# Norm steps only beside attention slots, a ring of five value quarters, six bias-table buffers, and bulk transfers on the Pool queue, in an eight-core transformer layer

## The chip, the cores and the metric

The kernel runs on all 8 cores of one Trainium2 chip; each core computes two of the sixteen sequences. The metric is the device time, in microseconds, of the slowest core. Cores 0 to 3 form die 0, cores 4 to 7 die 1. Some executions are slow on one die or on both, at a lower granted clock: in the profiled run of the kernel before, die 0 took 4469.6 us at a clock of 0.892, die 1 4179.2 us at 0.982.

## The reference, cut to what matters

One encoder layer: a gated feed-forward half step, two attention mixers side by side on one normalised input, a gated merge, a second feed-forward half step and a final norm.

```python
BATCH, SEQ, D_MODEL, D_FF = 16, 2048, 1024, 2816

def reference(x, ...):
    x = x + 0.5 * swiglu(rmsnorm(x, norm_ffn1[l]), ffn1_gate[l], ffn1_up[l], ffn1_down[l])
    h = rmsnorm(x, norm_mix[l])
    proj = h @ w_in[l]
    da_q, da_k, da_v, sw_q, sw_k, sw_v, gate = jnp.split(proj, splits, axis=-1)
    # ... lam from da_lambda ...
    o_da = diff_attention(...)      # dense, 8 heads of 2x64, ALiBi bias, values 128 wide
    o_sw = window_attention(...)    # band of +-128 tokens, 16 query heads, sink
    g = jax.nn.sigmoid(gate.reshape(B, S, 2, D_MODEL) + b_gate[l])
    merged = g[:, :, 0] * (o_da @ w_proj_da[l]) + g[:, :, 1] * (o_sw @ w_proj_swa[l])
    x = x + merged @ w_out[l]
    x = x + 0.5 * swiglu(rmsnorm(x, norm_ffn2[l]), ffn2_gate[l], ffn2_up[l], ffn2_down[l])
    return rmsnorm(x, norm_final)
```

## The kernel before

Activations lie as 8 blocks of 512 tokens (blocks 0 to 3 are the first sequence of the core, 4 to 7 the second). The program is a fixed list of stages. In the first half: GU (gate and up matmuls), D (down) and W (the projection), for pairs of blocks at first, then for single blocks. In the second half, per block: P (attention projections and gates), O (output projection), GU and D. I write O3 for block 3 in stage O. Blocks 4 to 7 pass through GU and D in both halves: below, GU4 to GU7 and D4 to D7 are those of the first half, and GU0 to GU3, D2 and D3 those of the second. The function `build` walks through *boundaries* between groups of matmuls. At each boundary it can put in three other kinds of work: an **attention slot**, a **norm step**, and the issue of **queued transfers** ("doling"). Attention runs in two spans, from the middle of W(2,3) to W7, and from W7 to P4.

```python
    def build(self):                        # cut
        span = [(at("W", (2, 3), 1) + 32, w7 + 12), (w7 + 18, at("P", (4,), 2) - 6)]
        for si, (k, bl, ph) in enumerate(st):
            inside = any(a <= n < b for a, b in span)
            self.gset = [6, 7] if inside else [6, 7, 0, 1, 2, 3, 4, 5]   # PSUM banks for the matmul groups
            self.rate = 2 if k == "D" and len(bl) == 1 else 1
            for _ in self.begin(k, bl, ph):
                n += 1
                # ...
                self.pre()                  # a norm step that needs the PE, if one is due
                for q, (a, b) in enumerate(span):
                    if n == a - (10, 6)[q]:
                        # ...
                        self.first_loads(q) # queues the first q, k, v, bias-table ... loads of a span
                    if a < n <= b:
                        want = int(total * (q + (n - a) / (b - a)) + 1e-6)
                        if done < want:
                            self.hint_group(k)          # the early wait, see below
                        while done < want:              # the attention slot
                            next(steps)
                            done += 1
                # ...
                self.post()                 # up to `rate` norm steps that need no PE
                self.dole()                 # issues queued transfers
            self.end(k, bl, ph)

    def hint_group(self, k):                # PE waits here for what the NEXT matmul group needs
        r, w = [], []
        t = "d" if k == "D" else "a"
        if self.taken[t] < self.issued[t]:
            r.append(("r" + t, self.taken[t] % self.nslot[t]))           # its weights
        if self.open is None:
            w.append(("bk", self.gset[self.gi % len(self.gset)]))        # its PSUM bank
        self.S.hint("pe", r, w)

    def dole(self):                         # dq[0]: attention's loads, dq[1]: everything else
        for _ in range(2 if len(self.dq[0]) > 2 else 1):
            q = self.dq[0] or self.dq[1]
            if q:
                q.pop(0)[1]()
```

A norm is a generator. Each `yield` is a step; `yield "pe"` announces a step that puts matmuls on the PE. If a stage needs the norm before its steps are used up, it is *drained*: all that is left runs at once and the PE waits for it.

```python
    def norm(self, ri, gi, hi=None, store=None, need=None):
        for c in range(8):                  # ACT squares, DVE sums: nacc
            # ...
            yield
        self.copy("dve", self.nh, self.nacc, ["nacc"], ["nh"])           # high and low bf16 parts
        self.tt(self.nl, self.nacc, self.nh, ALU.subtract, ["nacc", "nh"], ["nl"])
        yield
        yield "pe"
        b, bk = self.bank()
        # ... 8 matmuls of nh, nl with ones: sums over 128 partitions -> bank
        self.ts(self.ms, b[:, 0:4], 1.0 / 1024.0, 1e-6, ALU.mult, ALU.add, [bk], ["ms"])
        self.tt(self.r4, self.ms, self.mhalf, ALU.pow, ["ms", "mhalf"], ["r4"], eng="pool")
        # ... rh, rl = high and low parts of r4
        yield
        yield "pe"
        b, bk = self.bank()
        # ... 8 matmuls that broadcast rh, rl -> bank
        self.copy("act", self.nrb, b, [bk], ["nrb"])
        yield
        for c in range(8):                  # DVE: R * gain * nrb
            # ...
            yield

    def end(self, k, bl, ph):               # cut
        if k == "O" and b not in (3, 7):
            self.bg.append(self.norm(b % 2, 2, 0))
            if self.late:                   # final norms wait here for the next O
                self.bg += self.late
                self.late = []
        if k == "D":
            if b in (0, 1):
                self.late.append(self.normf(b))
```

Values and bias tables:

```python
    self.vD = sb("vD", [128, 16, 129], ...)               # one head's values, four quarters of 2x2 tiles
    def b_av(...):                                        # after the last use of a quarter by a head:
            if qb == 3 and c == 1 and u < 7:
                self.load_vD(sq, u + 1, bt)               # the next head's quarter goes to the same place

    self.tst = [sb("tst%d" % i, [128, 496], BF16, ...) for i in range(2)]
    for j in range(8):                                    # start of the program: 64 table pieces
        for h in range(8):
            self.act(self.tst[n % 2], self.dd, AF.Exp, ["dd"], [("tst", n % 2)], scale=-sl)
            self.dma(self.td_d[h][:, 496 * j:496 * (j + 1)], self.tst[n % 2], ...)
```

The softmax here doesn't subtract the row's maximum and nothing guards it: scores larger than these inputs give would overflow.

## Time and profile before

| quantity | before |
|---|---|
| time, median of 6 runs | 4199.47 us (4191.19 to 4222.8) |
| core 5: span, PE busy | 4183.4 us, 3932.1 us (94%) |
| core 5: PE idle before matmuls, all gaps summed | 242.4 us |
| core 5: time lost at half clock | 27 episodes, 81 us |

A half-clock episode is a stretch in which the clock record of the core stands at 0.5; half of its length is counted as lost. The views of waits below leave out gaps under 0.15 us.

The first view gives each core's span and mean granted PE clock. The profiled run was slow on die 0, so that die is not read.

```profile
core 5: 4183.4 us, clock 0.981
...
die 0 (median of its cores): 4469.6 us, clock 0.892
die 1 (median of its cores): 4179.2 us, clock 0.982
```

I read core 5: its trace holds all 27236 matmuls. From here on every profile line is of core 5 unless another is named. Its busy times (with share and instruction count), from the page:

```profile
PE 3932.1 (94%) x27236; PEld 2014.3 (48%) x27236; DVE 2374.2 (57%) x4565; ACT 1864.9 (45%) x2572; POOL 180.1 (4%) x247
```

PE bounds the kernel (it is busy for 94% of core 5's span and takes 76% of the chain that ended last), so I count a wait of PE's own as time on the critical path. The view of waits lists what ended them: total us, times, longest us.

```profile
PE bank L373 <- DVE nh L394: 32.3, 7, 10.4
...
PE bank L373 <- DVE of L382: 14.5, 3, 13.9
PE bank L373 <- DVE ms L388: 12.9, 13, 1.9
...
PE bank L373 <- DMA vD<-vd_d: 9.9, 5, 2.5
PE bank L373 <- ACT nrb L376: 9.2, 10, 1.0
...
PE bank L373 <- DMA H_64<-h_d: 8.5, 2, 7.8
...
PE bank L373 <- DMA qS<-qs_d: 2.2, 1, 2.2
```

The names: `nh` is the high part of a norm's sum of squares, `ms` its mean square, `nrb` the factor that the norm broadcasts, `of` a final norm's output, `vD` attention's values, `H` the normalised input, `qS` queries of the window mixer. The waits for `ms` and `nrb` come after norm steps. This is one of them in the timeline (start, us busy, engine, line, output and inputs; in brackets the idle time and what ended it):

```profile
2587.32 0.16 PE L373 MATMUL bank<-onesb,nh 128*128 128x1 bf16 x1 [1.02 <-DVE fr_79 L382]
...
2589.13 1.02 PE L373 MATMUL bank<-vD,et_104 128*128 128x129 bf16 x8 [1.46 <-DVE ms L388]
```

The sum matmuls start at 2587.32. The next thing that PE does is attention (`vD`, `et`), which has no use for `ms`. It waits all the same, since the early bank wait of `hint_group` stands ahead of the slot, and the bank is in use by the norm until `ms` has been read from it.

The 13.9 us wait for `of` is a drain. On DVE, at the head of stage O3:

```profile
2989.65 4.72 DVE L382 SCALAR_TENSOR_TENSOR R_62<-R_62,gains,nrb 128x512 f32<-128x512 f32 x7
3005.56 0.69 DVE L382 SCALAR_TENSOR_TENSOR R_62<-bank,R_62 128x512 f32<-128x512 f32 x1 [11.19 <-DMA R_62<-x_d]
```

Seven of the eight final multiplications of block 1's final norm run at once; only then can that buffer be stored and block 3's data be loaded into it, and DVE waits 11.19 us for the load.

For stages, the table of windows: window, its length, busy time of each engine (with counts), mean granted clock, DMA share, GB/s. A stage begins at the first matmul that uses a weight tile of that stage. DMA share is the mean busy share of the core's 16 DMA engines. The rows are the stages GU(0,1), W(2,3), P1, O1 and O3.

```profile
27.66:221.50 193.84, 165.16 (x721) 70.09 (x721) 78.06 (x128) 70.51 (x132) 12.98 (x23) 0.95 0.68 159
672.81:855.57 182.76, 175.34 (x1347) 102.64 (x1345) 90.44 (x174) 86.89 (x119) 11.09 (x18) 0.97 0.83 181
2228.95:2337.42 108.47, 95.41 (x767) 49.73 (x765) 70.47 (x140) 65.22 (x88) 3.37 (x3) 0.97 0.39 119
2530.55:2554.47 23.92, 22.75 (x187) 11.91 (x185) 17.95 (x40) 10.95 (x12) 1.01 (x1) 1.00 0.63 175
2987.23:3029.14 41.91, 26.62 (x206) 13.35 (x204) 24.32 (x49) 13.06 (x18) 1.01 (x1) 0.84 0.61 205
```

PE is busy only 165 of 194 us in GU(0,1), and 27 of 42 in O3. Finally, the sync engine's queue in W(2,3), where the first attention span begins (`kD` is attention's first load, `qS` the first load of queries for the window mixer):

```profile
717.15 1.39 SPq L401 DMA_DIRECT2D kD<-kd_d  x2
...
736.60 2.75 SPq L401 DMA_DIRECT2D vD<-vd_d  x2
...
747.32 0.46 SPq L401 DMA_DIRECT2D qS<-qs_d  x1
```

From the first load to `qS` it takes 747.32 − 717.15 = 30.2 us.

### The profile page before, as it was taken

To read this page: it belongs to the slowest core of one execution; us is meant where nothing else is said; L and a number is where in the kernel's file an instruction comes from. 1 tells how busy PE (TensorE), PEld (TensorE's weight loads), DVE (VectorE), ACT (ScalarE), POOL (GpSimd) and SP (SyncE) were. 2 spreads that over 40 slices of the span, in tenths; PEclk is the share of its full clock that TensorE was granted. 3 is DMA by queue.
4 is the path that set the end of the run, shared out by engine and by line. 5 is a ranking of instruction groups with operands and counts; after the bars stand their busy time and mean duration, and the time that the engine had idled before them with its cause. 6 is when DMAs were issued, how large, how long until landed. Compare 5 with 4: busy or idle time off the path is not lost.

```text
span 4509.8 us, 76897 instructions; the slowest of 8 cores (4170.2 to 4509.8 us)
## 1 busy us (share of the span) xinstructions
PE 4277.1 (95%) x27236; PEld 2123.1 (47%) x27236; DVE 2379.9 (53%) x4565; ACT 1867.9 (41%) x2572; POOL 180.2 (4%) x247
## 2 busy tenths in 40 slices
PE   7899999998998999999999999998989999999998
PEld 3344455544454454555444544444444444444443
DVE  4354234666676676664666466566656443343432
ACT  3422023665565565564555455454545211111111
POOL 1010000000000000000000000000000000000000
PEclk8999999999999999999988887887877888888887
DMA  7676698845697675568434335334333354354342
GB/s 174 162 159 173 145 202 182 184 138 142 152 229 174 155 187 154 149 180 212 141 108 137 105 101 172 102 108 137 109 105 120 118 190 154 121 192 159 125 140 92
DMA packets 295685, 675.26 MB, mean 150 GB/s; under 512 B 31216, under 2 KB 145264, under 8 KB 294640
## 3 DMA queue, kind: packets, MB, share of 16 engines
q1 hardware_dynamic: 279568, 602.42, 44.7%
q0 software_dynamic: 15744, 67.90, 9.9%
q8 instruction: 229, 3.75, 0.3%
q14 instruction: 144, 1.18, 0.1%
HBM read 605.09 MB, written 160.79 MB: 170 GB/s over the span
## 4 chain that ended last, share of the span: by engine, by line
PE 81%; DMA 7%; DVE 5%; issue 3%; ACT 2%; SPq 1%; POOL 0%; DVEq 0%; ACTq 0%; POOLq 0%
PE bank L373 80%; DMA vD<-vd_d 1%; SPq L401 1%; DMA td_d<-tst_146 1%; DMA td_d<-tst_145 1%; PE bank L1063 1%; DMA ra_67<-s_win 1%; DMA sw_d<-sst 1%; DVE nacc L379 0%; DMA ra_69<-s_win 0%; DVE osq L379 0%; DMA R_61<-x 0%; DMA s_win<-ra_66 0%; DMA rd_71<-s_d 0%; DVE R_61 L382 0%
## 5 line engine op out<-in xcount | busy, mean ns | idle before, releaser
L373 PE MATMUL bank<-H_63,ra_68 128*128 128x512 bf16 x976 | 255.8, 414 | 7.1 <-DVE H_63 L382 4.8
L376 ACT ACTIVATE et_102<-bank 128x1024 bf16<-128x1024 f32 x171 | 175.1, 1024 | 202.3 <-PE bank L373 200.3
L376 ACT ACTIVATE et_104<-bank 128x1024 bf16<-128x1024 f32 x171 | 175.2, 1024 | 195.6 <-PE bank L373 193.3
L376 ACT ACTIVATE et_106<-bank 128x1024 bf16<-128x1024 f32 x170 | 174.1, 1024 | 195.9 <-PE bank L373 193.5
L373 PE MATMUL bank<-H_63,ra_66 128*128 128x512 bf16 x912 | 239.7, 414 | 3.1 <-DVE H_63 L382 1.9
L373 PE MATMUL bank<-H_63,ra_70 128*128 128x512 bf16 x912 | 236.2, 412 | 3.6 <-DVE dn L379 3.6
L373 PE MATMUL bank<-H_63,ra_67 128*128 128x512 bf16 x912 | 237.9, 414 | 1.6 <-ACT nrb L376 0.8
L373 PE MATMUL bank<-H_63,ra_69 128*128 128x512 bf16 x928 | 237.2, 409 | 0.1
L379 DVE TENSOR_TENSOR et_104<-et_104,td 128x1024 bf16<-128x1024 bf16 x171 | 117.9, 689 | 151.1 <-ACT et_104 L376 150.7
L379 DVE TENSOR_TENSOR et_102<-et_102,td 128x1024 bf16<-128x1024 bf16 x171 | 117.8, 689 | 137.8 <-ACT et_102 L376 137.4
L379 DVE TENSOR_TENSOR et_106<-et_106,td 128x1024 bf16<-128x1024 bf16 x170 | 117.2, 689 | 132.9 <-ACT et_106 L376 132.5
L376 ACT ACTIVATE et_105<-bank 128x1024 bf16<-128x1024 f32 x171 | 174.1, 1018 | 0.0
L376 ACT ACTIVATE et_103<-bank 128x1024 bf16<-128x1024 f32 x171 | 174.0, 1018 | 0.0
L376 ACT ACTIVATE et_101<-bank 128x1024 bf16<-128x1024 f32 x170 | 173.0, 1018 | 0.0
L373 PEld LDWEIGHTS bank<-H_63,ra_68 128*128 128x128 bf16 x976 | 95.6, 104 | 155.4 <-issue 113.3
L379 POOL TENSOR_TENSOR rs_127<-ms_126,mhalf 128x4 f32<-128x4 f32 x64 | 69.3, 1082 | 2479.9 <-DVE ms_126 L382 2479.9
L373 PE MATMUL bank<-qD_93,kD 64*128 64x512 bf16 x1024 | 167.7, 409 | 0.5 <-DMA ra_69<-s_win 0.5
L373 PE MATMUL bank<-qD_94,kD 64*128 64x512 bf16 x1024 | 166.2, 405 | 0.0
L373 PE MATMUL bank<-aT_65,rd_73 128*128 128x512 bf16 x616 | 162.5, 419 | 0.5 <-ACT otS L376 0.5
L373 PE MATMUL bank<-aT_65,rd_71 128*128 128x512 bf16 x616 | 159.0, 412 | 0.9 <-ACT otD_107 L376 0.9
L373 PE MATMUL bank<-aT_65,rd_72 128*128 128x512 bf16 x616 | 159.0, 412 | 0.0
L373 PE MATMUL bank<-aT_65,rd_74 128*128 128x512 bf16 x616 | 159.0, 412 | 0.0
(313 smaller groups left out, 7982.8 us busy)
## 6 DMA issues: line engine op xcount, KB each, us to landing
ra_68<-s_gu SPq DMA_DIRECT2D x58, 512.0 KB, 3.8
ra_69<-s_gu SPq DMA_DIRECT2D x55, 512.0 KB, 3.7
ra_70<-s_gu SPq DMA_DIRECT2D x54, 512.0 KB, 3.5
ra_67<-s_gu SPq DMA_DIRECT2D x54, 512.0 KB, 3.7
ra_66<-s_gu SPq DMA_DIRECT2D x54, 512.0 KB, 3.9
rd_71<-s_d SPq DMA_DIRECT2D x52, 352.0 KB, 3.1
rd_73<-s_d SPq DMA_DIRECT2D x52, 352.0 KB, 3.3
rd_72<-s_d SPq DMA_DIRECT2D x48, 352.0 KB, 3.2
```

The source lines that it names most:

```text
L373: self.S.add("pe", lambda e: e.matmul(out, lhsT=lhsT, rhs=rhs, start=start, stop=stop), r=r, w=w)
L376: self.S.add("act", lambda e: e.activation(out=out, in_=in_, func=func, **kw), r=r, w=w)
L379: self.S.add(eng, lambda e: e.tensor_tensor(out=out, in0=a, in1=b, op=op), r=r, w=w)
L401: self.S.add(eng, lambda e: e.dma_start(out=out, in_=in_), r=r, w=w, dma=sem)
L1063: self.S.add("pe", lambda e, q=q: e.transpose(out=bt[:, q * 128:(q + 1) * 128], in_=src[:, q, :], identity=self.ident), r=[sk, "ident"], w ...
```

## The change

Its intent: remove those waits. Seven parts touch the time: (1) inside the attention spans a norm step with matmuls runs only at a boundary that has a slot, so that the slot's matmuls cover its latency; (2) one step more before the sum matmuls; (3) final norms are queued at once, and two steps run per boundary in O; (4) a ring of five quarters for the values, so that the next head's first quarter loads ahead; (5) six buffers for making the bias tables; (6) bulk transfers are issued from the Pool queue from the single-block stages on; (7) before those stages, doling happens only at every second boundary. In passing, the scheduler shares DMA semaphores among chains (not shown).

```diff
-        self.vD = sb("vD", [128, 16, 129], BF16, keys=([("vD", k) for k in range(8)], 516))
+        self.vD = sb("vD", [128, 5, 2, 2, 129], BF16, keys=([("vD", k) for k in range(5)], 1032))
-        self.tst = [... for i in range(2)]
+        self.tst = [... for i in range(6)]                     # and n % 2 -> n % 6 at its uses
@@ norm
         self.tt(self.nl, self.nacc, self.nh, ALU.subtract, ["nacc", "nh"], ["nl"])
+        yield
         yield
         yield "pe"
@@ later_dma
+            pool = q and self.bulk
+            self.dma(out, in_, r, w, (sem, "p") if pool else sem, eng="pool" if pool else "sp")
@@ load_vD, b_av
+    def vslot(self, sq, u, bt):
+        return (32 * sq + 4 * u + 3 - bt) % 5
-            if qb == 3 and c == 1 and u < 7:
-                self.load_vD(sq, u + 1, bt)
+            if qb == 3 and u < 7:
+                if c == 1 and bt:
+                    self.load_vD(sq, u + 1, bt - 1)
+                elif c == 0 and bt == 0:
+                    self.load_vD(sq, u + 1, 3)
@@ build
+            self.bulk = ph == 2 or len(bl) == 1
-            self.rate = 2 if k == "D" and len(bl) == 1 else 1
+            self.rate = 2 if k == "O" or k == "D" and len(bl) == 1 else 1
-                self.pre()
+                slot = False
+                for q, (a, b) in enumerate(span):
+                    if a < n <= b:
+                        slot = done < int(total * (q + (n - a) / (b - a)) + 1e-6)
+                if slot or len(self.gset) > 2:
+                    self.pre()
-                self.dole()
+                if self.bulk or n % 2:
+                    self.dole()
@@ end
-            if self.late:
-                self.bg += self.late
-                self.late = []
-                self.late.append(self.normf(b))
+                self.bg.append(self.normf(b))
[cut: semaphore chains in the scheduler; the table's access pattern]
```

## The prediction

The sum: +3 (−1 and +4), −9, −27, −18, −22, −10 and −3 make the 86 us of gain, and with 10 taken off for collisions about 77 remain (4199 to 4122 us).

> **What bounds it.** The page's run was slow on die 0, so I read die 1 (view of cores: clock 0.98, spans 4170 to 4188 us). TensorE bounds: 93% busy on core 4, 74% of its chain of waits; DVE 57%, ACT 45%. On cores 5 to 7 the waits before matmuls sum to 234 to 244 us. The clock records add 74 to 81 us lost in 22 to 27 half-clock episodes, mostly of 3.4 or 6.8 us, nearly all beside a wait of about 2 us or more; curing such a wait is worth about 1.7 us more. [...]
>
> **What the change does, on core 5 (view of waits; PE's own waits are critical).**
>
> 1. Norm PE steps only beside a slot: almost nothing by itself. After norm steps in an attention span PE waits 0.5 to 1.9 us (13 waits for ms, 12.9 us; 10 for nrb, 9.2 us), mostly already in front of attention matmuls, because the wait for the next group's bank is put ahead of the slot. That stays. Gain about 1 us. Norms get slower: counting steps, the drains before the GU stages of blocks 6 and 7 have two more steps left, cost about 4 us.
> 2. One step more before the sum matmuls: removes nh waits inside spans (2.1, 3.3, 0.6 us) and two episodes: about 9 us.
> 3. Final norms queued at once, two steps per boundary in O: counting steps, two drains go. One makes DVE wait 11.2 us for R_62<-x_d and PE 13.9 us, with a 13.7 us half-clock episode; the other costs 4.7 us. The norm drained between D of block 2 and GU of block 3 (nh 8.5 us, rh 1.8, 13.7 to 17 us episode) stays. Gain about 27 us.
> 4. Ring of five v quarters: removes vD<-vd_d waits (9.9 us; 10 to 19 over the cores) and their episodes: about 18 us.
> 5. Six table buffers: ACT waits 77 us for td_d<-tst, and PE about 23 us on fr between 75 and 220 us, with some five episodes: about 22 us. The sst waits (21 us of ACT) stay.
> 6. Bulk on the Pool queue: SP sits 8 us behind a weight slot before H_64<-h_d, PE waits 7.8 us plus a 6.8 us episode; a Pool issue takes 0.5 us and Pool is 4% busy. About 10 us. [...]
> 7. Halved doling before the single-block stages: DMA share there is 0.83 to 0.92; about 3 us.
>
> Semaphore chains: nothing.
>
> Sum about 86 us; I take off 10 for collisions (Pool's in-order waits ahead of the pow that attention needs, attention's first loads doled later): 4199 to about 4122 us.
>
> **To be seen if right:** vD, H_64<-h_d, "of" and tst waits vanish; nh shrinks to the first, last and block-3 drains; ms and nrb waits stay near 20 us together; about 12 episodes fewer, mean clock about 0.987; matmul busy time unchanged.
>
> **What would make it wrong:** rs waits on DVE growing because Pool waits for a bulk buffer; a norm missing its drain; new waits taking the freed time; or slot-only norm steps saving the ms and nrb waits after all, which would make it faster.
>
> Predicted 4122 us, 80% range 4088 to 4160; faster by over 2%: 0.42, within 2%: 0.56, slower: 0.02.

## The result, and the profile after

| quantity | before | after |
|---|---|---|
| time, median of all runs | 4198.73 us (20 runs, four of them above 4300) | 4175.28 us (10 runs, four of them slow) |
| ratio of fast runs | | 0.9911 (0.9889 to 0.9932) |
| core 5: span | 4183.4 us | 4141.3 us |
| core 5: PE idle before matmuls, all gaps summed | 242.4 us | 206.8 us |
| core 5: lost at half clock | 27 episodes, 81 us | 22 episodes, 71 us |

A ratio here is the mean time of one kernel's fast runs over the mean of the other's in the same rounds, so it is not quite the ratio of the medians quoted. 0.9911 of 4199 us is a gain of 37 us, within 2%. The prediction had 77 us. The six fast runs of after lie between 4151.06 and 4180.62 us, with a mean of 4161.8, just above the predicted range; the median over all ten is further above, because four were slow. On single dies that ran undisturbed (every core's clock above 0.972) the longest core took 4152.0 us, as the median of 18.

The cores' view of after (this run was fast on both dies) and core 5's busy times:

```profile
core 5: 4141.3 us, clock 0.983
...
die 0 (median of its cores): 4145.0 us, clock 0.983
die 1 (median of its cores): 4148.6 us, clock 0.983
```

```profile
PE 3924.6 (95%) x27236; PEld 2013.6 (49%) x27236; DVE 2372.2 (57%) x4565; ACT 1864.7 (45%) x2572; POOL 242.8 (6%) x359
```

The work is the same: equal counts on PE and DVE, and on Pool 112 instructions more, which are the issues of the bulk transfers (62.7 us more of busy time, 0.56 us each). PE's waits after:

```profile
PE bank L387 <- DVE nh L408: 23.7, 4, 8.5
...
PE bank L387 <- DVE ms L402: 13.0, 12, 1.7
PE bank L387 <- ACT nrb L390: 12.2, 12, 1.3
...
PE bank L387 <- DMA qS<-qs_d: 9.9, 1, 9.9
...
PE bank L387 <- DMA vD<-vd_d: 8.3, 1, 8.3
...
PE bank L387 <- DMA H_64<-h_d: 2.3, 2, 1.6
...
PE bank L387 <- DVE of L396: 0.5, 2, 0.3
```

`of` and `H` fell as predicted, and `nh` lost three of its seven waits (`rh`, the next wait of a norm, fell only from 20.0 us in 12 waits to 18.4 in 18). `ms` and `nrb` did not fall (22.1 us together before, 25.2 after), as the prediction's step 1 said. New are two single long waits, for `vD` and `qS`. The `vD` line keeps its size but not its nature: five waits at changes of head became one of 8.3 us. Both stand in one stage, W(2,3), as the windows of the same five stages show:

```profile
25.30:201.24 175.94, 162.96 (x720) 70.75 (x721) 81.75 (x133) 74.73 (x142) 13.42 (x24) 0.94 0.82 185
646.89:847.82 200.93, 176.98 (x1346) 103.48 (x1345) 90.14 (x174) 86.89 (x119) 11.05 (x18) 0.94 0.74 165
2201.66:2302.14 100.48, 94.04 (x767) 49.33 (x765) 70.35 (x140) 65.13 (x88) 3.76 (x3) 1.00 0.40 121
2495.27:2523.86 28.59, 24.84 (x195) 12.65 (x193) 23.25 (x52) 15.31 (x20) 2.36 (x2) 0.94 0.50 151
2954.14:2979.56 25.42, 24.33 (x203) 12.64 (x202) 19.19 (x41) 12.61 (x16) 2.13 (x3) 1.00 0.59 180
```

GU(0,1), P1 and O3 became 17.9, 8.0 and 16.5 us shorter. O1 became 4.7 us longer and W(2,3) 18.2 us longer. In W(2,3) the DMA share fell from 0.83 to 0.74, and the rate from 181 to 165 GB/s: the transfer engines had less to do while PE waited for transfers. The sync queue shows why:

```profile
693.13 1.15 SPq L415 DMA_DIRECT2D kD<-kd_d  x2
...
719.84 2.00 SPq L415 DMA_DIRECT2D vD<-vd_d  x2
...
740.21 0.52 SPq L415 DMA_DIRECT2D qS<-qs_d  x1
```

From attention's first load to `qS` it now takes 740.21 − 693.13 = 47.1 us, 16.9 more than before. The order of the loads is the same; they are handed out at half the rate. Between the values and `qS` the sync queue also sat 9.8 us behind a store of `sq_88`, a tile that only came after PE's wait for the values had ended: the first wait holds up the load for the second. PE's timeline puts its two waits beside these issues:

```profile
727.66 1.02 PE L387 MATMUL bank<-vD,et_102 128*128 128x129 bf16 x8 [8.31 <-DMA vD<-vd_d]
...
748.48 0.72 PE L387 MATMUL bank<-qS,kS 64*128 64x256 bf16 x4 [9.89 <-DMA qS<-qs_d]
```

PE began to wait for values at 727.66 − 8.31 = 719.35 us, and their first load was issued at 719.84. It began to wait for `qS` at 738.59, and that was issued at 740.21. In both cases PE stood there before the load had been issued.

For all stages I took the duration, as the median over the cores that are fast and have complete records (cores 5 to 7 of before; 0, 1, 3, 5, 6, 7 of after), in us. Waits quoted with these spans count those over 0.15 us.

| stages | before | after | change |
|---|---|---|---|
| GU(0,1) and D(0,1) | 276.2 | 256.8 | −19.4 |
| W(2,3) | 182.6 | 199.9 | +17.3 |
| GU4 to W7 | 1250.8 | 1234.0 | −16.8 |
| P1 | 108.2 | 99.3 | −8.9 |
| O1, P2, GU1, O2, P3, O3 | 442.0 | 427.2 | −14.8 |
| D3, P4, P5, P6 | 211.6 | 221.1 | +9.5 |
| sum over all stages | 4186.5 | 4144.8 | −41.7 |

### The profile page after: what moved, and what is told of

Read it like the earlier page. It is cut to its first block, busy times and chain, and to the rows that moved or that the text cites. A ratio compares the mean times of both kernels' runs of the same rounds, so it can differ in the third digit from the quotient of the medians.

```text
span 4152.7 us, 76918 instructions; the slowest of 8 cores (4136.9 to 4152.7 us)
## 1 busy us (share of the span) xinstructions
PE 3925.9 (95%) x27236; PEld 2014.7 (49%) x27236; DVE 2372.1 (57%) x4565; ACT 1864.7 (45%) x2572; POOL 243.0 (6%) x359
## 4 chain that ended last, share of the span: by engine, by line
PE 80%; DVE 7%; DMA 5%; issue 4%; ACT 2%; SPq 1%; POOL 1%; DVEq 0%; ACTq 0%; POOLq 0%
PE bank L387 79%; SPq L415 1%; DMA ra_66<-s_win 1%; DMA rd_71<-s_d 1%; PE bank L1090 1%; DMA vs_d<-ssv 1%; DMA sw_d<-sst 1%; DVE osq L393 1%; DVE nacc L393 1%; DVE of L396 1%; DMA H_64<-h_d 0%; POOL r_52 L393 0%; DVE aT_65 L393 0%; ACT et_101 L390 0%; DMA R_61<-x 0%
## 5 line engine op out<-in xcount | busy, mean ns | idle before, releaser
L387 PE MATMUL bank<-H_63,ra_68 128*128 128x512 bf16 x976 | 232.2, 383 | 9.1 <-DVE H_63 L396 6.3
L387 PE MATMUL bank<-H_63,ra_66 128*128 128x512 bf16 x912 | 216.4, 384 | 3.3 <-DVE H_63 L396 1.9
L387 PE MATMUL bank<-H_63,ra_69 128*128 128x512 bf16 x928 | 215.4, 380 | 0.1
L387 PE MATMUL bank<-H_63,ra_67 128*128 128x512 bf16 x912 | 214.2, 383 | 1.0 <-ACT nrb L390 0.8
L387 PE MATMUL bank<-H_63,ra_70 128*128 128x512 bf16 x912 | 211.6, 380 | 0.2
L387 PE MATMUL bank<-qD_93,kD 64*128 64x512 bf16 x1024 | 157.9, 387 | 2.4 <-DMA qD_93<-qd_d 2.4
L387 PEld LDWEIGHTS bank<-H_63,ra_68 128*128 128x128 bf16 x976 | 90.0, 98 | 138.7 <-issue 43.1
L387 PE MATMUL bank<-qD_94,kD 64*128 64x512 bf16 x1024 | 155.0, 381 | 0.0
L387 PEld LDWEIGHTS bank<-H_63,ra_66 128*128 128x128 bf16 x912 | 84.8, 98 | 124.0 <-issue 32.6
L387 PE MATMUL bank<-aT_65,rd_71 128*128 128x512 bf16 x616 | 142.3, 379 | 2.2 <-DMA rd_71<-s_d 1.3
L387 PEld LDWEIGHTS bank<-H_63,ra_69 128*128 128x128 bf16 x928 | 86.0, 98 | 119.2 <-issue 24.9
L387 PEld LDWEIGHTS bank<-H_63,ra_67 128*128 128x128 bf16 x912 | 85.3, 98 | 120.1 <-issue 28.1
```

The lines of the kernel that those rows point to most:

```text
L387: self.S.add("pe", lambda e: e.matmul(out, lhsT=lhsT, rhs=rhs, start=start, stop=stop), r=r, w=w)
```

## The experiments

Fifteen kernels ran, on four chips, each beside runs of the kernel before: a_dole, b_dole, b_slot and a_nohint on one chip; b_nohint, b_nohint_slot, a_nopool and a_rate1 on a second; b_vd, b_tab, a_best and a_best_sp on a third; b_norm, b_pool and b_step on a fourth. All gave correct results. An experiment named a_ edits the kernel after; one named b_ edits the kernel before. A ratio is always to the kernel before; a ratio in parentheses is its 95% interval. "Span" is the sum of the stage medians as in the table above. Where few runs were fast I also use undisturbed dies: of every run, fast or slow, each die whose four clocks were all above 0.972, with its longest core, and the median over these. One caution: the complete cores of before (5 to 7, one chip) had light `vD` waits, 9.9 to 18.6 us. Kernels with the old value buffer on other chips had 12.6 to 29.4 us (b_dole outside W(2,3) too), and their GU5, GU6 and GU7 are mostly 2 to 5 us longer under six different edits; I don't read those as effects of an edit.

Theory: halved doling (part 7) starves attention's first loads and costs about 17 us, and the rest of the shortfall is in the final norms (part 3) and the Pool queue (part 6). The rivals: the loads in W(2,3) are late for another reason, the Pool queue above all; the slot rule (part 1) costs more than it brings; and the extra steps in O only move waits.

### Doling alone: put back in after, added alone to before

```diff
 a_dole (from after)                       b_dole (from before)
-    if self.bulk or n % 2:               -    self.dole()
-        self.dole()                      +    if ph == 2 or len(bl) == 1 or n % 2:
+    self.dole()                          +        self.dole()
```

> After, with transfers doled at every boundary again. Theory (halved doling starves attention's first loads): the waits for vD and qS at the start of attention (8.3 and 9.9 us on core 5) shrink below 3 us together, the W stage of blocks 2 and 3 goes from 199.9 us back to about 183, and the kernel takes about 20 us less than after, ratio to before about 0.986. Rival (the waits come of the ring of v quarters or of the other transfers, not of doling): the W stage stays near 200 us and the ratio near 0.991.

> Before, with doling halved outside the single-block stages and the second phase, nothing else. Theory: the W stage of blocks 2 and 3 goes from 182.6 to about 199 us, with waits for vD and qS of some 8 and 10 us, ratio to before about 1.004. Rival: W stays near 183 us, ratio 1.000.

Measured: a_dole 0.9844 (0.9801 to 0.9886), b_dole 1.0052 (1.0027 to 1.0077). W(2,3) went from 199.9 to 184.0 us in a_dole, and from 182.6 to 200.8 in b_dole. In W(2,3) of b_dole, which has neither ring nor Pool queue nor slot rule, PE waits as in after:

```profile
PE bank L373 <- DMA qS<-qs_d: 9.8, 1, 9.8
PE bank L373 <- DMA vD<-vd_d: 9.7, 1, 9.7
```

In a_dole (core 1; its die was fast in this run) the `vD` wait is gone, 3.6 us for `qS` is left, and the DMA share of W(2,3) is back at 0.83:

```profile
651.80:837.45 185.65, 174.59 (x1347) 103.02 (x1345) 90.40 (x174) 87.03 (x119) 11.02 (x18) 0.97 0.83 179
...
PE bank L387 <- DMA qS<-qs_d: 3.6, 1, 3.6
```

The same edit moves the same stage by +18.2 and by −15.9 us, in both surroundings. The rivals for W(2,3) fall.

### The slot rule alone

```diff
 b_slot (from before)
-                self.pre()
+                slot = ...                      # as in the change
+                if slot or len(self.gset) > 2:
+                    self.pre()
```

> Before, with norm PE steps only at boundaries that hold a slot, nothing else. Theory (the wait for the next group's bank stands ahead of the slot, so the PE waits for the norm's result either way): ratio 0.998 to 1.003, and the waits for ms and nrb stay between 18 and 26 us together (22.1 before). Rival (the intent of the change: the slot covers the norm's latency): those waits fall below 8 us and the ratio is near 0.994.

Measured: 1.0023 (0.9994 to 1.0052); on undisturbed dies 4209.8 us (9) against 4202.6 (12). The waits that the rule aims at stay (before: 12.9 and 9.2):

```profile
PE bank L373 <- DVE ms L388: 12.2, 13, 1.7
...
PE bank L373 <- ACT nrb L376: 11.5, 12, 1.1
```

The norm step now always has a slot behind it, and the slot covers nothing. The prediction named the reason: the early bank wait. The next runs test that. (That the point estimate lies above 1 fits the 4 us that the prediction allowed for slower norms, but isn't clear of noise.)

### The early bank wait taken away

The hint is a wait for a buffer that the next group will wait for anyway, right before it writes.

```diff
 a_nohint (from after), b_nohint (from before), b_nohint_slot (b_nohint and the slot rule)
-        if self.open is None:
-            w.append(("bk", self.gset[self.gi % len(self.gset)]))
```

> After, with the early wait for the next group's bank taken out (the early wait for its weights stays). Theory: only then does a slot cover the norm's latency: the waits for ms and nrb (25 us together after) fall below 8 us, other waits grow by a few us, ratio to before about 0.986. Rival (the waits are attention's own and only end with ms and nrb): they change their name and the kernel's time does not move, ratio 0.991.

> Before, with the early wait for the next group's bank taken out, nothing else. Theory (the early wait itself costs most, with or without norm steps): the waits for ms and nrb fall but stay at the boundaries without a slot (about 6 of 24 steps, 4 to 8 us together), the waits for fr and aT in attention go too, ratio to before 0.984 to 0.989. Rival (the early wait costs nothing unless norm steps sit beside slots): ratio above 0.995.

> Before, without the early wait for the bank and with norm PE steps only beside a slot. Theory (a slot can cover the norm's latency once the early wait is gone): the waits for ms and nrb in the attention spans fall to 2 us or less together, some 5 us below the same kernel without the slot rule, ratio to before 0.982 to 0.988. Rival: no difference between the two in those waits.

Measured: a_nohint 0.9746 (0.9688 to 0.9803), b_nohint 0.9868 (0.9819 to 0.9916); b_nohint_slot has no ratio, since only two of its runs were fast (4132.72 and 4127.66 us); on undisturbed dies it took 4126.9 us (8) and b_nohint 4130.0 (8), against 4197.1 of before. The gain over after is 68 us by stages, where my theory had some 20 (0.986). In a_nohint the waits behind norm steps are all but gone (after: 13.0 and 12.2):

```profile
PE bank L387 <- ACT nrb L390: 0.8, 1, 0.8
...
PE bank L387 <- DVE ms L402: 0.6, 2, 0.3
```

The span of a_nohint is 68 us shorter than that of after (4144.8 to 4076.7): 45 us less PE waits (190.8 to 145.9), and 9 us less half-clock loss (67.0 to 57.6); the remaining 14 us I have not attributed. Thirteen of the 28 stages after W(2,3) up to P4 gain 2 to 9 us. Waits that no norm causes went too: on core 5, `aT` (an earlier group's result on its way out of the bank) fell from 11.5 us to 0.7, and `fr` (a work tile of the gates) from 29.8 to 12.0. In before, removing the two lines gives 74 us (4186.5 to 4112.6). So the early bank wait costs as much with the slot rule as without it, and my rival that it costs nothing by itself falls. With the wait gone, what remains for the slot rule is small: b_nohint and b_nohint_slot have equal spans (4112.6 and 4115.9), with `ms` and `nrb` waits on core 5 of 4.0 and 2.0 us. Covered or not, the norm steps' latency was mostly the price of the hint.

### The Pool queue: taken out of after, added alone to before

```diff
 a_nopool (from after)                     b_pool (from before): later_dma and self.bulk as in the change
-            pool = q and self.bulk
+            pool = False
```

> After, with the bulk transfers back on the SP queue. Theory: the wait for H_64<-h_d at the second P stage (7.8 us before, gone after) comes back with its half-clock episode, that stage goes from 99.3 to about 108 us, nothing else moves by more than 3 us, ratio to before about 0.993 to 0.994. Rival (the Pool queue saves more, by freeing SP for the weights): other stages grow too and the ratio is 0.996 or more.

> Before, with the bulk transfers on the Pool queue, nothing else. Theory (what it saves in one place it costs in others): the second P stage 7 to 9 us shorter, waits for weights in the W stages and in D of block 3 up by as much, ratio to before 0.999 to 1.002. Rival (the prediction's term): ratio 0.9975 or less.

Measured: a_nopool 0.9889 (0.9873 to 0.9904), b_pool 1.0012 (0.9956 to 1.0067). So the Pool queue gains nothing on balance, and both my theory for a_nopool (0.993 to 0.994) and its rival fell. For b_pool the fast runs hide a loss: two of the four fast runs of before in its rounds (4246.05 and 4227.19 us) had die 0 at a lower clock (0.960 to 0.975). On undisturbed dies b_pool took 4223.8 us (12 of them, scatter 0.13%) and before 4204.1 (13, 0.10%), 20 us longer with the Pool queue. In after the cost is smaller: by stages a_nopool is 7 us shorter (4144.8 to 4137.9). The stages show that it gains and loses. P1, where the loads of `H` and `oTa` sat behind a weight slot in the sync queue (7.5 us on core 5 of before, from 2213.48 to 2221.02), is 8.9 us shorter in after and 8.5 in b_pool; without Pool it is 6.0 longer than after. PE's waits for transfers, core 1 of after and then core 1 of a_nopool:

```profile
PE bank L387 <- DMA ra_66<-s_win: 11.7, 4, 4.5
...
PE bank L1090 <- DMA rd_71<-s_d: 3.5, 2, 2.6
```

```profile
PE bank L387 <- DMA oTa<-od_d: 4.5, 1, 4.5
PE bank L387 <- DMA H<-h_d: 2.9, 1, 2.9
```

The first fence is what the Pool queue brings: PE waits for *weight* tiles (`ra`, `rd`), which the sync queue still issues. In a_nopool no wait for `ra` or `rd` is left on this core, and in their place come the waits that Pool had removed, in the second fence. Core 1 is the clearest case. Over all eight cores of after the waits for `ra` and `rd` sum to 6.8 to 15.8 us; on the undisturbed die of a_nopool they are 9.3, 0, 8.9 and 0.2, and on that of before 0.9, 6.8, 6.3 and 0.5. So the mean falls by more than half, but not on every core. In b_pool the waits for values grow as well: 22.3 to 29.4 us for `vD` on its undisturbed die, where b_norm and b_step on the same chip have 13.8 to 23.5. In after the new ring has removed these waits outside W(2,3), which may be why the Pool queue costs less there; no run tests that. In stages: W4, W7 and D3 are 3.3, 8.9 and 4.1 us shorter in a_nopool (W7 on two of its three complete cores), P1 6.0 longer, P5 2.3 longer. Why the Pool queue gains nothing, and in b_pool costs 20 us, isn't shown. That the bulk transfers now run at a moment when a weight tile has to be loaded, and not later, is my reading of the swapped waits; no run shows the two transfers side by side.

### The extra norm steps in O, taken out of after

```diff
 a_rate1 (from after)
-            self.rate = 2 if k == "O" or k == "D" and len(bl) == 1 else 1
+            self.rate = 2 if k == "D" and len(bl) == 1 else 1
```

> After, with one norm step per boundary in the O stages as before. Theory (two steps per boundary fill DVE and delay its reads of the O stage's banks): the O stages of blocks 1 and 2 fall from 28.6 and 32.7 us to about 25 each, the P stages after them grow by 1 to 4 us each, two drains of one step come back, and the sum of O and P of these blocks is 5 us or so shorter; ratio to before 0.989 to 0.992. Rival (the O stages are longer only by the norm steps moved into them): the sum of O and P does not move by more than 2 us.

Measured: 0.9913 (0.9897 to 0.9928), the same as after. O1 and O2 got 3.4 and 6.5 us shorter, but GU1, P3 and P7 4.4, 7.8 and 3.2 longer. My theory, that the second step per boundary was a cost that could be saved, fell; the rival held, nearly: O1, P2, O2 and P3 together moved by −2.1 us and GU1 grew by 4.4, so the steps cost about the same where they land next.

### Ring, tables, final norms and the extra step, each alone on before

```diff
 b_vd   (from before): five-quarter ring, vslot, load_vD and b_av as in the change
 b_tab  (from before): six tst buffers
 b_norm (from before): rate 2 in O; final norms queued at once, no late list
 b_step (from before): one more `yield` ahead of the sum matmuls
```

> Before, with the ring of five quarters for v, nothing else. Theory (the prediction's term of 18 us): the waits for vD (10 to 19 us over the cores) fall below 4 us, 12 to 20 us shorter, ratio to before about 0.996. Rival (attention waits for other things at the same places): the vD waits go and others take their time, ratio 0.999 to 1.001.

> Before, with six bias-table buffers, nothing else. Theory: the first GU stage goes from 193.8 to about 176 us, nothing else moves by more than 3 us, ratio to before about 0.996. Rival (the change needs another part to gain there): the first GU stage stays above 188 us.

> Before, with the final norms queued at once and two steps per boundary in O, nothing else. Theory (the drains go, but the same norm steps now crowd DVE in the O stages): O of block 3 some 17 us shorter, GU of block 1 some 5 us, O of blocks 1 and 2 some 4 to 9 us longer each, P after them a little shorter: 12 to 16 us in all, ratio to before 0.996 to 0.997. Rival (the prediction's term, nothing given back): 24 us or more, ratio 0.994.

> Before, with one step more before the sum matmuls of a norm, nothing else. Theory (the prediction's term): the waits for nh inside the attention spans (6 us) and for nl go, the D stages of blocks 4 and 5 are 3 to 4 us shorter each, ratio to before about 0.998. Rival (the PE waits for something else at the same place): the D stages keep their length, ratio 1.000.

b_vd: 0.9928 (0.9903 to 0.9953). PE has no wait for `vD` left on core 5; GU4, GU5, GU6, GU7, D7, W7 and P1 are 2.4 to 4.3 us shorter each. Their sum, 24.6 us, is near the 30 us of the ratio; both are more than the 12 to 20 that I expected. The ring also takes away most of the `H` wait in P1 without any Pool queue (8.5 us on core 5 before, 0.9 here), so parts 4 and 6 overlap there.

b_tab: 0.9938 (0.9919 to 0.9958). GU(0,1) is 20.6 us and D(0,1) 4.9 us shorter, together 25.5, and the ratio gives 26. In before, ACT waited for two table buffers to be written out:

```profile
ACT tst_145 L376 <- DMA td_d<-tst_145: 44.3, 24, 7.4
ACT tst_146 L376 <- DMA td_d<-tst_146: 33.2, 13, 6.0
```

In b_tab this is 16.8 us in 11 waits, in after 1.1 us in three.

b_norm: 0.9954 (0.9883 to 1.0024), not clear of no change, since most runs on this chip were slow; on undisturbed dies 4194.1 us (8) against 4204.1 (13), 10 us shorter. By stages: O3 −16.9, GU1 −5.3, P2 −4.3, P3 −3.7, but O1 +9.9 and O2 +9.4, with O6 +2.4 and P7 −1.3; together about −10, a little under the 12 to 16 of the expectation. The two drains did go. What the prediction had left out is what their work costs in its new place. O1 went from 23.92 us (before) to

```profile
2529.37:2564.29 34.92, 28.16 (x203) 14.33 (x201) 24.92 (x54) 15.93 (x21) 2.36 (x2) 0.85 0.41 123
```

with 16 more matmuls (203 for 187), PE busy 5.4 us longer, and a clock of 0.85 where it had been 1.00.

b_step: one fast run only (4210.85 us), so no ratio. On undisturbed dies it took 4204.4 us (8) and before 4204.1 (13): no change. By stages (the three complete cores of the fast die): D4 −4.1, D5 −4.0, D2 −2.5 (the first two as expected), but P2 +2.3, P3 +3.5, P7 +4.0, and 1.3 to 1.6 each in P4, P5 and P6: a sum near zero (+3.5). So the D stages did get shorter, and the total still did not. The step cures the wait ahead of the sum matmuls; the norm, one step longer, then reaches its later steps in other places.

### A version that beats both

```diff
 a_best (from after)
-                if self.bulk or n % 2:
+                if self.bulk or n % 2 or self.dq[0]:    # attention's loads are never held back
                     self.dole()
 hint_group: the two bank lines removed
 begin, second half, "GU":
-            self.drain()
+            if b != 3:                                   # final norm of block 2 may run on
+                self.drain()
 a_best_sp: the same, with pool = False
```

> After, with: transfers doled at every boundary while attention's own loads wait in the queue; no early wait for the next group's bank; the final norm of block 2 left to run beside the GU stage of block 3 instead of before it. If the three add up: 15 us less in the W stage of blocks 2 and 3, 65 us less over the attention spans, and some 18 us less at the end of the D stage of block 2 (72.7 to about 57 us), so a span of about 4047 us, ratio to before 0.966. If they overlap (the same waits counted twice): 0.972 or more.

> The same as a_best with the bulk transfers on the SP queue. Theory (the Pool queue saves the wait for H_64 in the second P stage, 6 us, but brings the transfers down on the weights of the W stages, which costs 10 us or so): 3 to 8 us shorter than a_best. Rival (the Pool queue is a gain): 5 us or more longer than a_best.

Measured: a_best 0.9693 (0.9642 to 0.9744), lowest 4053.58 us; a_best_sp 0.9669 (0.9629 to 0.9709), lowest 4052.59 us. Against after, a_best_sp is at an estimated 0.9669 / 0.9911 = 0.976, from two sets of rounds. The span of a_best is 4048.0 us, where 4047 stood in the expectation if the three add up: in sum they do. W(2,3) is back at 181.5 us, and D2 is 14.6 us shorter than after, since the norm of block 2 no longer has to be drained. Which queue is better for the bulk can't be told from the two ratios (the intervals overlap); by stages the sync queue is 7 us shorter (4040.6), as the theory had it. But not because the weight waits go: `ra` and `rd` sum to 10.2 to 15.6 us over the cores of a_best and to 2.8 to 17.9 in a_best_sp. Only those in D3 are gone in both kernels without the Pool queue. PE waits 122.7 and 114.7 us in the spans, after 190.8.

## Why the prediction was right or wrong

By part, in us; minus is a gain. "In after" is what the stages of after show; "alone" is from the kernel with that part alone.

| part | predicted | in after | alone |
|---|---|---|---|
| 1 slot rule, with slower norms | +3 (−1 and +4) | `ms`, `nrb` waits not shorter | 0 to +10 (1.0023) |
| 2 step before the sum matmuls | −9 | three `nh` waits fewer | 0 on undisturbed dies |
| 3 final norms | −27 | −15 | −10 by stages and on undisturbed dies |
| 4 value ring | −18 | −17 for GU4 to W7, parts 2 and 6 included | −25 to −30 (0.9928) |
| 5 six table buffers | −22 | −19 | −26 (0.9938) |
| 6 Pool queue | −10 | P1 −9, given back; +7 in all by stages | +20 on undisturbed dies (1.0012) |
| 7 halved doling | −3 | W(2,3) +17 | +18 in its stage (1.0052) |
| collisions | +10 | | |

**Right.** Part 1: "That stays." The slot rule brings nothing, because the early bank wait is put ahead of the slot; b_slot shows that it brings nothing, and a_nohint that it is this wait. (Without the wait the rule brings 2 us less of `ms` and `nrb` waits and no shorter span, so it was hardly needed.) Parts 4 and 5 gave what was predicted, or a little more. The counting of drains was right: two went and the one at block 2 stayed (`nh` 8.5 us, still the longest `nh` wait of after).

**The step that failed** first is part 7, whose sign was wrong: "Halved doling before the single-block stages: DMA share there is 0.83 to 0.92; about 3 us." I read a high DMA share as congestion, and so took fewer transfers per boundary as relief. But the same queue hands out attention's first loads, and the first span begins inside a two-block stage. Halving the rate stretched (on core 5) the time from the first load to `qS` from 30.2 to 47.1 us, and PE waited 8.3 and 9.9 us for loads that had not yet been issued, with half-clock episodes beside them (23.9 us at half clock in W(2,3) of core 5, after 10.2 before). The DMA share *fell*, to 0.74. The prediction names the danger ("attention's first loads doled later"), but inside a lump of 10 us for all collisions, unsized. It could have been sized from what was known: 20 loads stand ahead of `qS`, two go per boundary, and W(2,3) has 72 boundaries in 182.6 us, 2.5 us each. That is an estimated 25 us at every boundary and 51 at every second one (30.2 and 47.1 were measured; a load that a slot needs is issued at once). The runs give about +17 us in place of −3, a miss of 20 us.

**Three terms mis-sized.** Part 3 was credited with the whole length of the two drains (27 us). O3 did get 16.9 us shorter and GU1 5.3, but the same steps now run in O1 and O2 and cost 4.7 and 8.5 us there; net 15 in after, about 10 alone. Part 6 was credited with the 8 us wait and its episode in P1. P1 gave them, but W4, W7 and D3 took them back, in part by new waits for weight tiles: 10 to 17 us over. Part 2 was credited with 9 us for the waits that it removes, and nothing for the later steps of all other norms, which it moves too: alone about 0.

Together: 20 (part 7), 12 to 17 (part 3), 10 to 17 (part 6) and 9 (part 2) make 51 to 63 us too much. Against that stand 11 to 16 us that parts 4 and 5 gave beyond the prediction when alone, and the 10 us allowed for collisions; part 1 is left out, since its ratio allows a small loss too. The net is 25 to 42 us, where the shortfall is 77 − 37 = 40; the sum mixes stages of after with parts tested alone, and can't be closer than that. The six ratios measured alone multiply to 1.0023 · 0.9954 · 0.9928 · 0.9938 · 1.0012 · 1.0052 = 0.991, which is that of the whole. But that is luck: each of them is known to a few tenths of a per cent only, b_step has none, and the medians of undisturbed dies of all seven multiply to 0.997, against 0.987 to 0.990 for the whole (4152.0 us over the 4193.1 to 4204.1 of before on the four chips). So by these medians the parts don't simply multiply: together they gain some 30 us more than alone, and which of them work together is open.

**The half-clock state.** The prediction counted 1.7 us of clock (half of the shortest episode, 3.41 us) for each cured wait of about 2 us, and some 12 episodes fewer. Five fewer were seen, since new waits bring their own: in W(2,3) the clock loss rose from 3.4 to 11.9 us (medians over the cores). Part of that runs during the waits themselves (PE is idle in 11.7 of those 23.9 us on core 5), so it can't simply be added to them. In the traces of core 5, before and after, every episode but the last is 3.41 us long or a multiple of it, at a factor of exactly 0.5, and all start on one grid of 3.413 us. On core 5 of before, 21 of 27 began with less than 3.0 us of idle PE in the 3.4 us ahead of them, one with 1.49 us. Counted by steps of that grid (from 20 us on, at full clock; the nine complete cores of before and after used for stages), no step with under 1.49 us of idle PE was followed by an episode, and every one with over 2.04 us was; in between it went either way. That is a count over two runs, not a rule.

In the profiled run of before, the clock records of the four cores of die 0, the slow one, hold 2135 to 2295 us at 0.8125. In that of after, which was fast on all eight cores (PE 95% busy on core 5), no core's records hold any time at that value, and the means are 0.982 to 0.985. So it is a state of some runs, not of all; what brings it on isn't shown.

**Open.** Why the weight loads come late with the Pool queue (contention, or the order in which buffers come free) isn't shown, nor why the Pool queue alone costs 20 us and in after about 7. That part 2 alone is worth about nothing rests on one fast run, on eight undisturbed dies and on the stages of three cores.

## What to carry to other kernels

When a queue feeds two consumers, size a change of its rate at the moment when the more urgent one starts: count its first loads times the boundaries each takes; a high DMA share (0.83 here) doesn't tell that fewer issues are harmless (the stage took 17 to 18 us more). A wait put early "because it has to be waited for anyway" can undo what should cover a latency: look at what PE does right after it, and try the kernel without the hint before building around it (here two lines were worth 68 to 74 us, more than the whole change). When a drain disappears, credit only the difference to what its steps cost where they run next (in b_norm 22.2 us off O3 and GU1, and 19.3 on O1 and O2).
